# Hybrid DeltaNet / attention layer on one core: small merge matmuls in four unbroken runs a head, and an order planned with transfer issue times, one more dependence and eight transfers under way

## The chip, the core and the metric

The kernel runs on one core of a Trainium2 chip. The metric is the device time of one execution in microseconds (us), the median of several. Engines are called as the profile does: PE (TensorE matmul), PEld (its weight loads), DVE (VectorE), ACT (ScalarE), POOL (GpSimd) and SP (SyncE, which only issues transfers; ACT issues some too).

## What is computed

One layer over 1024 latent tokens and 256 context tokens of width 1024, all in 32-bit floats. Two branches are fed from one projection and merged by gates:

```python
a_mat = jnp.where(strict, einsum('nbhid,nbhjd->nbhij', kc * bc[..., None], kc) * decay, 0.0)
t_mat = lax.linalg.triangular_solve(eye + a_mat, eye, left_side=True, lower=True)
u = t_mat @ (vc * bc[..., None])
w = t_mat @ (kc * (bc * jnp.exp(gc))[..., None])
def step(s, xs_i):                       # one chunk after the other
    v_new = u_i - einsum('bhck,bhkv->bhcv', w_i, s)
    s_next = s * jnp.exp(gl_i)[..., None, None] + einsum('bhck,bhcv->bhkv', kd_i, v_new)
    o = einsum('bhck,bhkv->bhcv', qd_i, s) + einsum('bhij,bhjv->bhiv', qk_i, v_new)
...
o_b = diff_attend(q_l, concatenate([k_c, k_l]), concatenate([v_c, v_l]), lam)   # 8 heads, softmax
merged = g_a * (y_a @ w_oa) + g_b * (y_b @ w_ob)
return x + gate * (merged @ w_out)
```

Branch A is a gated delta rule, in both directions, for 8 heads. Each head needs, for every chunk, the inverse of a triangular matrix, and then a scan over the chunks. Branch B is softmax attention.

## The kernel before

The kernel works with chunks of 128 tokens, 10 a head and direction. Its stages follow each other on PE: the projection and its convolution (to some 430 us of the span), the query, key and value parts of attention with the preparation of the first two heads of the delta rule (to 756 us), the two scans of the delta rule with the rest of the preparation (to 1350 us), attention together with the projection `ma` of branch A (to 1832 us), and the last projections `mb`, `x`, `z`.

**Preparation of a head** (`gdn_prep`, line 1077 on). `gram` products and decays give the matrix `X`. Its 32x32 blocks on the diagonal go through DRAM (`da`, read back as `ab`), are inverted by 62 steps on DVE in the tile `ts` (lines 1153 and 1155), which POOL first sets to zeros and ones (lines 1146 and 1147), and are stored as `db` (line 1157, issued by SP) and read back as `RR`. Then blocks are merged, by four kinds of small matmul: 40 of 32x32 into `pz`, 60 of 32x32 into `p2` and `p3`, and, for each half of the chunks, 10 of 64x64 into `pz6` and 10 into `pu6`. A PSUM pool of two banks (`gpa`) serves these, `gram`, and the transposes `tr` and `oT`. The profile writes the tiles as `pz`, `p` and `pu`; each of these matmuls stands in the trace as two passes, as those of `chain`, `out` and `gram` do.

**Scans** (`scan`, line 1289 on). For each of two directions: `chain` matmuls on PE, scalings on ACT (`vd`, line 1318, `vn`) and DVE (`r`, line 1309, `S`, line 1331), in a ring of dependence; `out` matmuls beside it. `sets` (line 1265) loads a head's `sk`, `kk`, `vv` and `sq`, `loads` (line 1280) the `x` and `qk` of two chunks. `tails` finishes a head: `of` and the product `oa` (line 1387) on POOL, then the transposes `oT` on PE.

**Fill.** Where no scan or preparation has a matmul ready, PE is given `mm` matmuls of other projections (`fill_flow`, units of 48 matmuls of 128x512); their outputs `zo` leave PSUM on ACT (line 1031), which then issues their transfer (line 1033).

**What sets the order.** The program is written in the order that a planner in the kernel's own code finds: every part is a generator that yields an engine, a cost in us and what it waits for; `flow` (and `turn_flow` for the front and for attention) takes the part that could start first by the planner's clocks, with a bias for each part (`BIAS`, `WB`, `ABIAS`; a lower one goes first). The engines work in order, so what the planner puts ahead on an engine is waited for there.

Of the kernel before, what the change touches and what calls it, by code (L numbers as in the profile page):

```python
# [23 lines left out]
NT = LT // P  # L24
# [19 lines left out]
class Block:  # L44
    def __init__(self, ctx, tc, a):
        self.ctx, self.tc, self.nc, self.a = ctx, tc, tc.nc, a
        self.dbg = {}
        self.now = self.dq = 0.0
        self.clk, self.port = [0.0] * 5, [0.0, 0.0]
        self.table, self.heat = None, 0.0  # L50
        self.streams = []
        self.ahead = None

    def mm(self, out, lhsT, rhs, start=True, stop=True):
        self.nc.tensor.matmul(out, lhsT, rhs, start=start, stop=stop)  # L55

# [56 lines left out]
    def begin_at(self, e, ready):  # L113
        return max(self.clk[ENG[e]], ready, self.port[1] if e == DV2 else self.port[0] if e == POOL else 0.0)
# [6 lines left out]
    def step(self, s):  # L121
# [588 lines left out]
    def run(self):  # L710
# [4 lines left out]
        with ExitStack() as left:  # L715
            self.hp, self.hs = self.spool(left, "hp"), {}
            self.hgroup(0)
            with ExitStack() as lw, ExitStack() as cx:
# [21 lines left out]
                with tc.manual_schedule(engines={E.PE, E.DVE, E.Activation, E.Pool, E.SP}):  # L740
# [30 lines left out]
                    for g, b in ((self.scan(0), 0), (self.scan(1), 0), (self.forever(self.outq[0]), 1),  # L771
                                 (self.forever(self.outq[1]), 1), (self.forever(self.evacs), 2),
                                 (self.forever(self.posts[0]), 2), (self.forever(self.posts[1]), 2), (first, 3),
                                 (self.preps(1), 3), (self.tails(), 3), (self.sets(), 3), (self.loads(0), 3), (self.loads(1), 3),
                                 (self.forever(self.asides), 3)):
# [263 lines left out]
    def gdn_first(self):  # L1039
# [8 lines left out]
        self.unit_t = {}  # L1048
# [28 lines left out]
    def gdn_prep(self, h):  # L1077
# [68 lines left out]
        t1 = yield PL1, 0.89, [], lambda: nc.gpsimd.memset(ts, 0.0)  # L1146
# [10 lines left out]
        t = yield DMA, 0.91, [t], lambda: nc.sync.dma_start(self.db[h].rearrange("u m i j -> (u m) i j"), ts)  # L1157
# [24 lines left out]
        for c in range(NT):  # L1182
            for (b1, b2) in ((0, 1), (2, 3)):
                t = yield PE, 0.03, [tz, b], lambda: self.mm(p2[B(b1), c], R[B(b1), c], Z[B(b1), c]), 0.25
                t = yield PE, 0.03, [tz, b], lambda: self.mm(p2[B(b2), c], Rt[B(b2), NT + c], Z[B(b2), c]), 0.25
            t3 = yield PE, 0.02, [tz, b], lambda: self.mm(p3[B(1), c], Z[B(0), c], R[B(0), c]), 0.25
            t3 = yield PE, 0.02, [tz, b], lambda: self.mm(p3[B(2), c], Z[B(3), c], Rt[B(3), NT + c]), 0.25
# [17 lines left out]
        ends = []  # L1205
        for c0, nb in ((5, 5), (0, 5)):
            cs = slice(c0, c0 + nb)
            yield self.psum()
            b = self.banks.pop(0)
            pz = PT("pz6")[:, :nb * 64].rearrange("p (c f) -> p c f", f=64)  # L1210
            for j in range(nb):
                c = c0 + j
                t = yield PE, 0.065, [tx, b], lambda: self.mm(pz[lo, j], X[hi, 0, c, lo], X[hi, 0, c, hi]), 0.5
                t = yield PE, 0.065, [tx, b], lambda: self.mm(pz[hi, j], X[lo, 1, c, hi], X[lo, 1, c, lo]), 0.5
            tz = yield DVE, 0.398, [t], lambda: V.tensor_scalar_mul(Z6[:, cs], pz, -1.0)
# [989 lines left out]
```

## Time and profile before

| what | value |
|---|---|
| time, median of 3 runs | 2006.67 us (2004.43 to 2008.17) |
| profiled execution: its own time | 2004.12 us |
| its span, first to last instruction | 2002.3 us |
| PE busy | 1940.0 us (97%) |
| PEld busy | 1692.7 us (85%) |
| DVE, ACT, POOL busy | 1457.0, 1071.5, 673.9 us |
| mean granted clock of TensorE | 0.992 |

The profiled execution's own time is 1.8 us above its span. Ends of matmuls are modelled by the profiler, so the time from start to start tells more of PE than its busy time.

### The profile page before, as it was taken

The numbers are of one execution on the slowest core, as the hardware profiler recorded it, in microseconds if no ns is written. First come the engines' busy times: TensorE is split into PE (matmuls) and PEld (weight loads), VectorE is DVE, ScalarE is ACT, GpSimd is POOL, SyncE is SP. The second block draws the span as 40 slices with busy tenths as digits, with TensorE's granted clock in tenths as the row PEclk, the third lists the DMA queues.
The fourth block names the chain that finished last, engine by engine and source line by source line (L and its number), as shares of the span: only waits on it lengthen the run. The fifth ranks groups of instructions, "written<-read, shape, count | busy, mean of one in ns | idle before, by whom it ended". The sixth has DMA issues, their size and how long they took to land.

```text
span 2002.3 us, 37575 instructions
## 1 busy us (share of the span) xinstructions
PE 1940.0 (97%) x13807; PEld 1692.7 (85%) x13807; DVE 1457.0 (73%) x3613; ACT 1071.5 (54%) x2187; POOL 673.9 (34%) x610
## 2 busy tenths in 40 slices
PE   6999999999999999999899999999999999999999
PEld 4988888899999997878777888887788888888887
DVE  4797989858877895557556786237679999885677
ACT  4453445352325543666456754547668888874222
POOL 3200000015521422332323333334657666672203
PEclk9999999999999999999999999999999999999999
DMA  9154453575456645855664765648664575336542
GB/s 323 59 145 108 132 131 95 134 228 165 129 158 211 195 152 147 260 178 193 194 224 133 257 173 164 218 140 249 169 163 117 148 232 140 108 107 211 189 157 85
DMA packets 388415, 336.40 MB, mean 168 GB/s; under 512 B 144913, under 2 KB 331891, under 8 KB 388231
## 3 DMA queue, kind: packets, MB, share of 16 engines
q1 hardware_dynamic: 324295, 273.18, 46.3%
q10 hardware_dynamic: 63936, 60.83, 9.8%
q8 instruction: 109, 1.79, 0.4%
q14 instruction: 75, 0.61, 0.1%
HBM read 222.14 MB, written 111.79 MB: 167 GB/s over the span
## 4 chain that ended last, share of the span: by engine, by line
PE 73%; DVE 10%; DMA 8%; ACT 4%; issue 2%; SPq 1%; POOL 1%; ACTq 0%; DVEq 0%; POOLq 0%
PE mm L55 37%; PE chain L55 5%; PE v L55 5%; PE mb L55 4%; PE s L55 4%; PE ma L55 3%; PE x L55 3%; DVE S L1560 3%; PE out L55 3%; PE t L58 2%; DMA hx<-in_w_in_dram 1%; PE gram L55 1%; DVE al L1634 1%; ACT S L1573 1%; DVE ac L590 1%
## 5 line engine op out<-in xcount | busy, mean ns | idle before, releaser
L55 PE MATMUL mm<-hs,wh 128*128 128x512 f32 (+1 forms) x2048 | 648.9, 391 | 1.5 <-DVE hs L403 1.4
L55 PEld LDWEIGHTS mm<-hs,wh 128*128 128x128 f32 x2048 | 373.1, 190 | 60.3 <-DVE hs L403 2.0
L55 PE MATMUL mm<-hs,wl 128*128 128x512 f32 (+1 forms) x1024 | 400.8, 391 | 0.0
L55 PE MATMUL mm<-wh,hs 128*128 128x256 f32 (+1 forms) x1792 | 334.8, 286 | 0.0
L55 PEld LDWEIGHTS mm<-wh,hs 128*128 128x128 f32 x1792 | 281.5, 191 | 0.4
L1560 DVE TENSOR_SCALAR_CACHE_REDUCE S<-s,rsq 128x512 f32<-128x512 f32 (+1 forms) x384 | 241.9, 655 | 33.6 <-PE s L55 30.8
L55 PE MATMUL mm<-wl,hs 128*128 128x256 f32 (+1 forms) x896 | 256.0, 286 | 0.0
L55 PEld LDWEIGHTS mm<-hs,wl 128*128 128x128 f32 x1024 | 194.9, 190 | 29.1 <-issue 0.9
L1597 POOL TENSOR_TENSOR S<-S 128x1280 f32<-128x1280 f32 x64 | 188.8, 2952 | 90.2 <-ACT S L1590 87.7
L1573 ACT ACTIVATE S<-S,mn 128x1280 f32<-128x1280 f32 x128 | 174.7, 1366 | 34.5 <-DVE mn L1572 33.7
L55 PEld LDWEIGHTS mm<-wl,hs 128*128 128x128 f32 x896 | 171.2, 191 | 0.3
L590 DVE SCALAR_TENSOR_TENSOR ac<-xc,convT,ac 128x1284 f32<-128x1284 f32 (+1 forms) x96 | 138.7, 1449 | 16.3 <-ACT ac L588 15.6
L55 PE MATMUL s<-kk,qh 128*128 128x512 f32 (+1 forms) x384 | 145.3, 379 | 3.1 <-DVE S L1560 2.8
L55 PE MATMUL s<-kk,ql 128*128 128x512 f32 (+1 forms) x384 | 134.0, 360 | 0.0
L1634 DVE TENSOR_TENSOR al<-t,ah 128x512 fp32r<-128x512 f32 (+1 forms) x192 | 107.6, 593 | 10.3 <-ACT ah L1629 9.7
L1629 ACT CAST ah<-t 128x512 fp32r<-128x512 f32 (+1 forms) x192 | 90.0, 516 | 30.4 <-PE t L58 29.1
L575 POOL MEMSET xc<- 128x2 f32 (+1 forms) x64 | 3.6, 99 | 301.8 <-DMA gkk<-xc 118.0
L1153 DVE TENSOR_TENSOR tmp<-ab,ts 80x31 f32<-80x31 f32 (+15 forms) x248 | 97.2, 392 | 8.2 <-DMA ab<-da 2.6
L1331 DVE SCALAR_TENSOR_TENSOR S<-S,egl,chain 128x128 f32<-128x128 f32 x128 | 43.1, 344 | 79.8 <-PE chain L55 76.8
L578 ACT COPY xc<-mm 128x512 f32<-128x512 f32 (+1 forms) x64 | 33.4, 534 | 125.2 <-PE mm L55 101.7
L58 PE MATMUL t<-ct,S 128*128 128x128 f32 x640 | 95.8, 276 | 1.0 <-ACT zo L1031 0.5
L1318 ACT ACTIVATE vd<-chain,edk 128x128 f32<-128x128 f32 x144 | 52.2, 369 | 80.4 <-PE chain L55 75.0
(298 smaller groups left out, 4478.1 us busy)
## 6 DMA issues: line engine op xcount, KB each, us to landing
wr<-in_w_in_dram ACTq DMA_DIRECT2D x44, 512.0 KB
hx<-in_w_in_dram ACTq DMA_DIRECT2D x64, 256.0 KB
X<-gcd SPq DMA_DIRECT2D x16, 640.0 KB
kd<-col SPq DMA_DIRECT2D x40, 256.0 KB
xd<-X SPq DMA_DIRECT2D x16, 640.0 KB
x<-xd SPq DMA_DIRECT2D x80, 128.0 KB
kk<-kd SPq DMA_DIRECT2D x32, 320.0 KB
wa<-in_w_ada_dram SPq DMA_DIRECT2D x8, 1024.0 KB
```

The costliest lines, as they stand in the source:

```text
L55: self.nc.tensor.matmul(out, lhsT, rhs, start=start, stop=stop)
L58: self.nc.tensor.transpose(out, src, self.ident[:src.shape[0], :src.shape[0]])
L578: e = yield ACT, 0.57 if m == 512 else 0.31, [t, x["old"]], lambda: nc.scalar.copy(xc[:, d:d + m], pt[:, :m])
L590: t = yield DV2, 1.21e-3 * wd, [t], lambda: nc.vector.scalar_tensor_tensor(ac[:, :wd], xc[:, j:j + wd], self.convw(j, x["ct"]), ac[:, :wd] ...
L1153: t = yield DV2, n * w / 960.0 + 0.08, [t, t1], lambda: V.tensor_tensor(tv, ab[:, j + 1:, j:j + 1].to_broadcast([80, n, w]), ts[:, j, :w]. ...
L1318: td = yield ACT, 0.251, [t], lambda: nc.scalar.activation(vd, pc[:, 1], AF.Copy, scale=self.edk[:, c, g:g + 1])
L1331: t = yield DVE, 0.263, [t], lambda: V.scalar_tensor_tensor(Sn, S, self.egl[:, c, g:g + 1], pc[:, 2], ALU.mult, ALU.add)
L1560: e = yield DVE, 0.675 if m == 512 else 0.408, [e, self.sfree[c].get(n - 4 + c)], lambda: self.nc.vector.tensor_scalar(x["S"][c][:, o:o + ...
L1573: x["x"].append((yield ACT, 1.36, [e], lambda: nc.scalar.activation(S, S, AF.Exp, bias=x["mn"][:, c:c + 1], scale=-1.0, accum_out=w["l0"][ ...
L1597: e = yield POOL, 2.9, [e], lambda: self.nc.gpsimd.tensor_tensor(S0, S0, S1, ALU.add)
L1629: e = yield ACT, 0.48 if nb == 4 else 0.27, [t, y["old", k]], lambda: self.nc.scalar.copy(y["ah", k][:, :, q], pv)
L1634: t = yield DVE, 0.603 if k < 2 else 0.322, [e, y["old", k]], lambda: self.nc.vector.tensor_tensor(y["al", k][:, :, q], pv, y["ah", k][:, ...
```

## The change

The 40 matmuls into `pz`, the 60 into `p2` and `p3`, the 20 into `pz6` and the 20 into `pu6` of a head are each yielded as one piece, with one cost, so that the planner can put nothing between them; the two halves of the 64x64 steps are done together, which takes both banks of the pool at a time (`psum(2)`). The planner's model gets three terms: an issue on SP takes 0.4 us of SP instead of 0.05; a transfer is not issued before the eighth transfer back has landed (`lanes`; this holds for issues by SP and by ACT); and the zeroing of `ts` waits for the last store of `ts` (`ts_t`). `sets` loads `vv` and `kk` ahead of `sk`, and in the first head all but `vv` come after the first loads of both scans. Biases are changed: `sets` goes from 0 to -0.3, `loads` from 0 to -0.5, the fill's weights from -0.3 to -0.15, and in attention several of `ABIAS`. (`FB1` is changed too, but it is used only where 38 units of fill are done, and there are 32.)

```diff
@@ class Block
+        self.lanes = [0.0] * 8
+    def mms(self, ops):
+        for x in ops:
+            self.mm(*x)
...
     def begin_at(self, e, ready):
-        return max(self.clk[ENG[e]], ready, self.port[1] if e == DV2 else self.port[0] if e == POOL else 0.0)
+        return max(self.clk[ENG[e]], ready, self.port[1] if e == DV2 else self.port[0] if e == POOL else
+                   self.lanes[0] if e in (DMA, ADMA) else 0.0)
...
-            self.clk[e] = start + 0.05 if h[0] == DMA else keep
+            self.clk[e] = start + self.SPI if h[0] == DMA else keep
             end += self.LAND
+            self.lanes = self.lanes[1:] + [end]
@@ gdn_prep
-        t1 = yield PL1, 0.89, [], lambda: nc.gpsimd.memset(ts, 0.0)
+        t1 = yield PL1, 0.89, [self.ts_t], lambda: nc.gpsimd.memset(ts, 0.0)
...
-        t = yield DMA, 0.91, [t], lambda: nc.sync.dma_start(self.db[h].rearrange("u m i j -> (u m) i j"), ts)
+        t = self.ts_t = yield DMA, 0.91, [t], lambda: nc.sync.dma_start(self.db[h].rearrange("u m i j -> (u m) i j"), ts)
...
-        for c in range(NT):
-            for (b1, b2) in ((0, 1), (2, 3)):
-                t = yield PE, 0.03, [tt, b], lambda: self.mm(pz[B(b1), c], X[B(b2), 0, c, B(b1)], Rt[B(b2), c]), 0.25
-                t = yield PE, 0.03, [tt, b], lambda: self.mm(pz[B(b2), c], X[B(b1), 1, c, B(b2)], R[B(b1), NT + c]), 0.25
+        t = yield PE, 1.02, [tt, b], lambda: self.mms(
+            x for c in range(NT) for b1, b2 in ((0, 1), (2, 3)) for x in (
+                (pz[B(b1), c], X[B(b2), 0, c, B(b1)], Rt[B(b2), c]), (pz[B(b2), c], X[B(b1), 1, c, B(b2)], R[B(b1), NT + c]))), 0.25
...
-        for c0, nb in ((5, 5), (0, 5)):
-            cs = slice(c0, c0 + nb)
-            yield self.psum()
-            b = self.banks.pop(0)
...
+        yield self.psum(2)
+        b = [self.banks.pop(0), self.banks.pop(0)]
+        pz = [v6("pz6"), v6("pz6")]
+        t = yield PE, 1.5, [tx, b], lambda: self.mms(
+            x for cs, z in zip(halves, pz) for j in range(5) for c in (cs.start + j,) for x in (
+                (z[lo, j], X[hi, 0, c, lo], X[hi, 0, c, hi]), (z[hi, j], X[lo, 1, c, hi], X[lo, 1, c, lo]))), 0.5
...
@@ sets
-            for n, src in (("sk", self.gk[h]), ("kk", self.gkk[h]), ("vv", self.gv[h]), ("sq", self.gq[h])):
+            for n, src in (("vv", self.gv[h]), ("kk", self.gkk[h]), ("sk", self.gk[h]), ("sq", self.gq[h])):
+                if h == 0 and n == "kk":
+                    yield lambda: all((d, 0, 8) in self.units_ for d in range(2))
@@ biases
+    SPI = 0.4
-    WB = -0.3
+    WB = -0.15
-    BIAS = (0, 0, -0.3, 0, 0)
+    BIAS = dict(scan=0, outq=0, evacs=-0.3, posts=-0.3, preps=0, tails=0, sets=-0.3, loads=-0.5, asides=0)
-    ABIAS = dict(rels=-5.0, softs=-5.7, norms=3.8, gateq=-13.3, sums=-15.8,
-                 outs=-32.1, lows=-2.4, highs=-13.2, adds=30.9, scales=31.0, evs=-3.0, mouts=13.8,
-                 att_out=0.5, turns=5.3, scores=-2.6, merge=1.0)
+    ABIAS = dict(rels=-5.0, softs=-0.02, norms=6.65, gateq=-13.3, sums=-14.54,
+                 outs=-50.16, lows=-2.4, highs=-2.68, adds=26.02, scales=31.0, evs=22.29, mouts=13.8,
+                 att_out=-3.61, turns=3.19, scores=-6.47, merge=1.0)
```

The same instructions are issued before and after, but for four more table loads on ACT (33 instead of 29). What moves is seen at three places.

On PE, at the first merge that falls into the scans (head 2; `pz` is the merge, `chain` and `out` the scans, `mm` the fill). Before:

```order
L55 MATMUL pz<-RR,X 32x32 x3
L55 MATMUL chain<-S,sk 128x128
L55 MATMUL pz<-RR,X 32x32 x2
L55 MATMUL chain<-r,x 128x128
L55 MATMUL pz<-RR,X 32x32 x18
L55 MATMUL out<-S,sq 128x128
L55 MATMUL pz<-RR,X 32x32 x2
L55 MATMUL chain<-r,x 128x128
L55 MATMUL pz<-RR,X 32x32 x9
L55 MATMUL chain<-vd,kk 128x128
L55 MATMUL out<-vn,qk 128x128
L55 MATMUL out<-S,sq 128x128
```

The same merge now:

```order
L56 MATMUL chain<-S,sk 128x128
L56 MATMUL mm<-hs,wl 128x512
L56 MATMUL out<-S,sq 128x128
L56 MATMUL mm<-hs,wh 128x512
L56 MATMUL pz<-RR,X 32x32 x40
L56 MATMUL chain<-r,x 128x128
L56 MATMUL chain<-vd,kk 128x128
L56 MATMUL out<-vn,qk 128x128
```

Six pieces of `pz` with scan matmuls between them have become one piece of 40. Over the whole program the small matmuls stood in 111 pieces before (26 of `pz` 32x32, 36 of `p`, 21 of `pz` 64x64 and 28 of `pu`), and stand in 32 now (8 of each).

On POOL, where the sixth zeroing of `ts` (MEMSET, `L1146` before) meets the third head's end (`of`, then `oa<-oa,of`). Before:

```order
L1282 TENSOR_TENSOR qk<-qk,ct 128x256 x2
L172 TENSOR_TENSOR of<-of,mhalf 128x8
L1146 MEMSET ts 80x1024
L1387 TENSOR_TENSOR oa<-oa,of 128x1024
L880 TENSOR_TENSOR wl<-hx,wh 128x512
L1147 MEMSET ts 80x32
```

Now:

```order
L179 TENSOR_TENSOR of<-of,mhalf 128x8
L1394 TENSOR_TENSOR oa<-oa,of 128x1024
L887 TENSOR_TENSOR wl<-hx,wh 128x512
L1153 MEMSET ts 80x1024
L1154 MEMSET ts 80x32
L1289 TENSOR_TENSOR qk<-qk,ct 128x256 x4
```

The zeroing has gone from ahead of the product `oa` to behind it and behind a weight's split `wl`.

On SP, at the start of the scans (`qd` and `qkd` are stores of the stages before). Before:

```order
L1018 DMA qd<-col 128x2x256 x4
L1265 DMA sk<-gk 128x1280
L1265 DMA kk<-gkk 128x10x128
L1265 DMA vv<-gv 128x10x128
L1265 DMA sq<-gq 128x1024
L1280 DMA x<-xd 128x256 x2
L1280 DMA qk<-qkd 128x256
L1280 DMA x<-xd 128x256 x2
```

Now:

```order
L1025 DMA qd<-col 128x2x256 x2
L1287 DMA x<-xd 128x256 x2
L1287 DMA qk<-qkd 128x256
L1287 DMA x<-xd 128x256 x2
L1287 DMA qk<-qkd 128x256
L1272 DMA vv<-gv 128x10x128
L1272 DMA kk<-gkk 128x10x128
L1272 DMA sk<-gk 128x1280
```

The small loads of both scans go out ahead of the four large ones, of which `vv` is now the first and `sk` the third.

Of the 2688 fill and projection matmuls `mm` of 128x512, 1224 stood ahead of the first `chain` and 87 behind the last `oT`; now 1208 and 133 do, and behind the first score matmul of attention stand 90 instead of 39.

## Rows read from the trace of the kernel before

**Rows 1.** The span and the mean granted clock of the core.
```profile
core 0: 2002.3 us, clock 0.992
```

**Rows 2.** Busy time by stage: stretch of the span, its length, then busy us (and instructions) of PE, PEld, DVE, ACT and POOL, the granted TensorE clock, the share of the DMA engines and GB/s.
```profile
0.00:100.00 100.00, 81.88 (x570) 65.92 (x571) 59.85 (x98) 47.46 (x76) 28.01 (x48) 1.00 0.55 191
100.00:430.00 330.00, 328.19 (x1767) 282.70 (x1766) 275.90 (x413) 142.12 (x181) 3.85 (x55) 1.00 0.52 133
430.00:756.00 326.00, 323.28 (x3106) 316.66 (x3105) 263.03 (x671) 139.80 (x314) 117.47 (x89) 1.00 0.56 175
756.00:1350.00 594.00, 569.92 (x4689) 483.54 (x4688) 349.70 (x992) 331.16 (x957) 188.69 (x248) 0.98 0.61 189
1350.00:1440.00 90.00, 82.53 (x444) 68.97 (x443) 59.53 (x200) 60.36 (x94) 42.68 (x21) 0.94 0.79 213
1440.00:1832.00 392.00, 387.87 (x2523) 339.87 (x2522) 334.80 (x1113) 309.64 (x516) 256.29 (x129) 1.00 0.54 150
```

**Rows 3.** What PE waited for between 756 and 1350 us: us in total, times, longest.
```profile
PE chain L55 <- ACT vd L1318: 9.7, 3, 4.9
PE oT L58 <- POOL oa L1387: 5.3, 1, 5.3
PE chain L55 <- DMA qk<-qkd: 3.3, 1, 3.3
...
PE chain L55 <- DMA vv<-gv: 1.8, 2, 1.6
```

**Rows 4.** PE in order of time around an unbroken merge (head 0): start us, us from the first start to the last end of the row, instruction and count (of passes).
```profile
588.31 0.28 PE L55 MATMUL mm<-wl,hs 128*128 128x256 f32 x1
588.43 0.28 PE L55 MATMUL mm<-wh,hs 128*128 128x256 f32 x1
588.64 0.89 PE L55 MATMUL pz<-RR,X 32*32 32x32 f32 x80
589.45 0.38 PE L55 MATMUL mm<-wh,hs 128*128 128x256 f32 x1
589.68 0.28 PE L55 MATMUL mm<-wl,hs 128*128 128x256 f32 x1
```

**Rows 5.** The same view around a merge that is cut into pieces (head 2).
```profile
782.87 0.49 PE L55 MATMUL chain<-S,sk 128*128 128x128 f32 x2
783.29 0.25 PE L55 MATMUL pz<-RR,X 32*32 32x32 f32 x4
783.47 0.49 PE L55 MATMUL chain<-r,x 128*128 128x128 f32 x2
...
785.98 0.39 PE L55 MATMUL out<-vn,qk 128*128 128x128 f32 x2
786.20 0.39 PE L55 MATMUL out<-S,sq 128*128 128x128 f32 x2
```

**Rows 6.** POOL in order of time; in brackets the idle time before and what ended it.
```profile
959.89 1.65 POOL L172 TENSOR_TENSOR of<-of,mhalf 128x8 f32<-128x8 f32 x1 [6.41 <-DVE of L1384]
969.94 0.95 POOL L1146 MEMSET ts<- 80x1024 f32 x1 [8.40 <-DMA db<-ts]
970.85 1.90 POOL L1387 TENSOR_TENSOR oa<-oa,of 128x1024 f32<-128x1024 f32 x1
```

**Rows 7.** SP in order of time: issue of transfers (start us, us, which).
```profile
748.54 3.74 SPq L1265 DMA_DIRECT2D sq<-gq  x1
...
957.88 7.17 SPq L1139 DMA_DIRECT2D da<-X  x4
...
966.28 0.60 SPq L1157 DMA_DIRECT2D db<-ts  x1
```

**Rows 8.** ACT in order of time.
```profile
893.87 0.34 ACTq L1033 DMA_DIRECT2D sza<-zo  x1
894.26 2.44 ACT L1231 ACTIVATE X<-X,beta 128x128 f32<-128x128 f32 x8 [5.60 <-DMA sq<-gq]
...
1130.38 2.45 ACT L1102 ACTIVATE X<-X,gcc 128x128 f32<-128x128 f32 x8 [0.69 <-ACT zo L1031]
1132.85 1.28 ACT L1104 ACT_TABLE_LOAD   x1
```

**Rows 9.** Stretches in which the granted clock was half, in the columns of the second group.
```profile
758.60:765.40 6.80, 5.58 (x16) 4.74 (x17) 0.29 (x1) 1.76 (x4) 0.00 (x0) 0.50 0.76 184
898.50:901.90 3.40, 3.40 (x27) 2.84 (x27) 0.70 (x2) 0.00 (x0) 3.03 (x4) 0.50 0.94 300
970.20:977.00 6.80, 4.20 (x14) 3.72 (x15) 0.69 (x2) 0.00 (x0) 4.52 (x5) 0.50 1.12 210
1055.50:1058.90 3.40, 3.40 (x25) 2.58 (x23) 1.79 (x5) 2.80 (x9) 1.23 (x1) 0.50 0.00 0
1383.20:1386.60 3.40, 3.40 (x12) 2.64 (x12) 3.03 (x11) 3.40 (x6) 0.65 (x1) 0.50 0.84 268
1431.00:1437.80 6.80, 5.11 (x18) 4.43 (x19) 4.36 (x14) 4.43 (x11) 4.98 (x3) 0.50 0.50 154
```

**Rows 10.** What PE waited for between 1350 and 1440 us, the longest one.
```profile
PE v L55 <- DVE mn L1572: 4.7, 1, 4.7
```

**Rows 11.** What PE waited for between 1440 and 1832 us, the longest one.
```profile
PE s L55 <- DVE S L1560: 1.0, 3, 0.4
```

More of the change, by code (lines that the diff above doesn't have):

```diff
@@ L770, in more @@
                         yield lambda: False
[L771 to L775, printed above, removed]
+                    for g, b in ((self.scan(0), "scan"), (self.scan(1), "scan"), (self.forever(self.outq[0]), "outq"),
+                                 (self.forever(self.outq[1]), "outq"), (self.forever(self.evacs), "evacs"),
+                                 (self.forever(self.posts[0]), "posts"), (self.forever(self.posts[1]), "posts"), (first, "preps"),
+                                 (self.preps(1), "preps"), (self.tails(), "tails"), (self.sets(), "sets"), (self.loads(0), "loads"),
+                                 (self.loads(1), "loads"), (self.forever(self.asides), "asides")):
                         self.stream(g, self.BIAS[b]) if g is not first else self.streams.append([g, self.BIAS[b], head, None])
@@ L1204, in gdn_prep @@
         Z6 = T("Z6", [P, NT, 64], "w4")
-        ends = []
-        for c0, nb in ((5, 5), (0, 5)):
-            cs = slice(c0, c0 + nb)
-            yield self.psum()
-            b = self.banks.pop(0)
[L1210 to L1215, printed above, removed]
-            self.banks.append(tz)
-            yield self.psum()
-            b = self.banks.pop(0)
-            pu = PT("pu6")[:, :nb * 64].rearrange("p (c f) -> p c f", f=64)
-            for j in range(nb):
-                c = c0 + j
-                t = yield PE, 0.065, [tz, t6, b], lambda: self.mm(pu[lo, j], t64[lo, c], Z6[lo, c]), 0.5
-                t = yield PE, 0.065, [tz, t6, b], lambda: self.mm(pu[hi, j], t64[hi, c], Z6[hi, c]), 0.5
-            e = [(yield PL1, 0.38, [tz], lambda: nc.gpsimd.memset(X[hi, 0, cs, lo], 0.0)),
-                 (yield PL1, 0.38, [tz], lambda: nc.gpsimd.memset(X[lo, 1, cs, hi], 0.0))]
-            f = [(yield ACT, 0.43, [t], lambda: nc.scalar.copy(X[lo, 0, cs, hi], pu[lo])),
-                 (yield ACT, 0.43, [t], lambda: nc.scalar.copy(X[hi, 1, cs, lo], pu[hi]))]
@@ new lines, in gdn_prep @@
+        tz = []
+        for cs, z in zip(halves, pz):
+            tz += [(yield DVE, 0.398, [t], lambda: V.tensor_scalar_mul(Z6[:, cs], z, -1.0))]
+            self.banks.append(tz[-1])
+        yield self.psum(2)
+        b = [self.banks.pop(0), self.banks.pop(0)]
+        pu = [v6("pu6"), v6("pu6")]
+        t = yield PE, 1.5, [tz, t6, b], lambda: self.mms(
+            x for cs, u in zip(halves, pu) for j in range(5) for c in (cs.start + j,) for x in (
+                (u[lo, j], t64[lo, c], Z6[lo, c]), (u[hi, j], t64[hi, c], Z6[hi, c]))), 0.5
@@ L1228, in gdn_prep @@
+        for cs, u in zip(halves, pu):
+            e = [(yield PL1, 0.38, tz, lambda: nc.gpsimd.memset(X[hi, 0, cs, lo], 0.0)),
+                 (yield PL1, 0.38, tz, lambda: nc.gpsimd.memset(X[lo, 1, cs, hi], 0.0))]
+            f = [(yield ACT, 0.43, [t], lambda: nc.scalar.copy(X[lo, 0, cs, hi], u[lo])),
+                 (yield ACT, 0.43, [t], lambda: nc.scalar.copy(X[hi, 1, cs, lo], u[hi]))]
             self.banks.append(f)
+            ends = []
             for d in range(2):
-                for c in range(c0, c0 + nb):
-                    t = yield ACT, 0.263, [e, f], lambda: nc.scalar.activation(
+                for c in range(cs.start, cs.stop):
+                    t1 = yield ACT, 0.263, [e, f], lambda: nc.scalar.activation(
```

18 lines of the change are left out of this document (9 added, 9 removed).

## The prediction

> **What bounds the kernel now.** I read the stages first [rows 2]. In each of them PE is busy for nearly the whole stretch: 328.2 of 330 us in the convolution, 323.3 of 326 in the parts of attention, 387.9 of 392 in attention. PE has work of its own everywhere, because fill is put wherever a scan or a softmax is late, so the time is PE's work plus the time in which PE stands still or is clocked down. The two weak stretches are the scans (569.9 of 594 us, granted clock 0.98) and the start of attention (82.5 of 90 us, clock 0.94). The front (81.9 of 100 us) keeps its order.
>
> Then I read what PE waited for in the scans [rows 3], and, for each wait, what the engine that was waited for had been doing [rows 6 to 8]. The reader should see that these waits do not come from the scans' own arithmetic but from an engine that was held, in order, by something else. At 970 us PE waits 5.3 us for POOL's product `oa`; POOL has been standing 8.4 us before its zeroing of `ts`, for the store `db`; and SP issued `db` late, at 966.28 us, because four issues of `da` had kept it 7.17 us [rows 6, 7]. At 894 us ACT waits 5.6 us for the landing of an unrelated load, `sq`, behind which it could issue a store of its own and only then go on to `vd`, for which the scan waits [rows 3, 8]. At the scans' start SP needs 3.74 us to issue one load of 512 KB [rows 7], and PE waits 3.3 us for a load issued behind it [rows 3]. Last I read the clock: it was at its lower level, 1.2 GHz, in six stretches in and after the scans, 30.6 us in all, and the four of the scans, from 758.6, 898.5, 970.2 and 1055.5 us on, are as many as the waits of PE there that were longer than 3 us; in the third PE was busy for only 4.2 of 6.8 us [rows 3, 9].
>
> **The change, part by part.** The sum is made against the profiled execution: span 2002.3 us [rows 1], 2004.1 us by its own time, which is 2.6 us below the median of the runs.
>
> *Fewer pieces.* An unbroken merge of 80 passes takes the fill from start to start from 588.43 to 589.68 us, 1.25 us for two matmuls that alone take 0.12 us each (588.31 to 588.43): 1.01 us for 80 passes [rows 4]. A piece of 4 passes between two scan matmuls takes these from 782.87 to 783.47, 0.60 us where scan matmuls without a piece between them follow after 0.22 (785.98 to 786.20): 0.38 us for 4 passes [rows 5]. So (1.01 - 0.38) / 76 = 0.008 us is what a pass costs, and 0.38 - 4 x 0.008 = 0.35 us is what a piece costs by itself, whatever is in it: PE goes over from the full array to the small blocks and back, and the matmuls on both sides are late. The order has 111 pieces before and 32 now. 79 x 0.35 = -27.7 us, all of it time of PE, and fill takes it up at once. For the 46 of these cuts that are of 32x32 the price is measured; the other 33 are of 64x64, and their price is taken from the same row. Ends: 46 x 0.35 = -16 us if a cut of 64x64 costs nothing, and -36 us if it costs 0.6 us, the whole of the gap in row 783.47.
>
> *Planned with issue times, the store's dependence and eight transfers.* In the scans PE stood still for 594 - 569.9 = 24.1 us [rows 2]; the four stretches at half clock there last 20.4 us [rows 9], of which PE was busy 16.6, so that they cost some 8 us. Together 32 us. The three new terms are the causes that the rows show: the zeroing that held POOL (5.3 us, and with it 6.8 us of half clock), the issues on SP (3.3 and 1.8 us, and 6.8 us of half clock), and ACT's issue that waits for a landing (9.7 us in three waits, and twice 3.4 us of half clock). The order now has the zeroing behind `oa`, and the scans' first loads ahead of the large ones. But the planner still takes 0.4 us for any issue where one took 3.74 us and four took 7.17, and an order with other waits may bring others. I take half: -16 us. Ends: nothing, and -32 us.
>
> *Merges that cannot be broken.* A scan matmul that becomes ready during one now waits for up to 1.0 us, as long as the measured one takes [rows 4], and may wait longer for 64x64. 24 of the 32 pieces, those of six heads, lie in the scans. That costs nothing as long as fill is there: PE works through the merge. The cover is real: 133 `mm` of 128x512 are left behind the last `oT`, against 87 before. If it were gone, half of 24 x 1.0 us, 12 us, would come back.
>
> *Start of attention.* PE stood still for 7.5 us in 1350 to 1440 us [rows 2], 4.7 of them in one wait behind DVE's queue [rows 10], and 10.2 us ran at half clock [rows 9], some 4 us. Now 90 instead of 39 matmuls of fill are left to put into these gaps. I take a third: -4 us, with ends 0 and -11.
>
> *Attention itself.* PE stood still for only 4.1 us, and its longest kind of wait sums to 1.0 us [rows 2, 11]: nothing can be won, and a new order of an engine that is busy 334.8 of 392 us (DVE) can lose. I take +4 us, about what PE now stands still there; ends -3 and, as the rival below, much more.
>
> *Table loads on ACT.* Four more at 1.28 us [rows 8], 5 us of an engine that is busy 331 of 594 us in the scans: 0, and +5 if every one of them holds up a `vd` that PE waits for. The Trainium skill (ScalarE: Activation LUTs, section "What ACT_TABLE_LOAD costs") adds about 1.38 us of drain to each load, by which four would be some 10.6 us, an estimate from that page, and the sum 1973 if all of it were on the path. The trace does not agree: the load at 1132.85 us starts 0.02 us after the work before it ends [rows 8].
>
> Sum: -27.7 - 16 - 4 + 4 = -43.7 us, 2004.1 to 1960.4 us, and with the 2.6 us of the median **1963 us**.
>
> **The rivals.**
>
> *The counts do not fit the chip.* The merges pay, but the planner's new waits are as wrong as the old: as many us of standing still in the scans as before, elsewhere. For it: issues of 1.8 us and more, which 0.4 us does not tell of [rows 7]. Against it: the largest single waits are just those that the three terms name. Then 2006.7 - 27.7 = 1979 us.
>
> *The scans set the pace.* PE is not the limit between 756 and 1350 us but the ring of `chain`, ACT and DVE; then PE time that is saved turns into waiting, and unbroken merges hold the ring up. For it: weight loads keep PEld busy for only 483.5 of 594 us there, 81%, against 97% in the stage before [rows 2]. Against it: PE's waits there sum to 24 us, and it always has fill. Then the 27.7 us are lost, which leaves 2006.7 - 16 - 4 + 4 = 1991 us, or with the 12 us of merges on top about 2003 us, no change. The Trainium skill (Perfetto Trace Analysis, section "Identifying the Most-Contended Engine") holds that busy time of matmuls is a poor measure of how full PE is, and busy time of weight loads a good one. By that rule this rival would be the likelier; scan matmuls that follow each other without a gap (0.22 us from start to start for one of two passes) speak against it [rows 5].
>
> *Attention is slowed: slower than before.* `evs`, DVE's emptying of score banks, goes from -3 to +22.29 in the biases, behind nearly all else on DVE, which is busy 85% of that stage [rows 2]. A score matmul then finds no free bank and PE, in order, stands. The place is the score matmuls `s`; the price of a stall as the one at the start of attention is 4.7 us of standing [rows 10] and half of the 5.1 us that PE worked at half clock from 1431 us on [rows 9], 7 us a time. Six such stalls, fewer than one a head, eat the 44 us; with twelve the time is 1963 + 84 = 2047 us. Against it: PE now gets its scores in smaller portions between `t` and `ma`, which gives DVE time to empty the banks.
>
> *It does not do what it says.* If the order had hardly moved, the time would stay at 2006.7 us; the order on PE speaks against it.
>
> **How the numbers follow.** 1963 us as the sum has it, between 1944 and 1974: 0.56. The counts that do not fit, 1974 to 1990 us: 0.2. The scans' pace: 0.12, of which two thirds fall near 1991 us and one third at no change. Attention slowed: 0.1. Nothing done: 0.02. The range from 1944 to 1992 us takes in the forecast, the second case and most of the third. Its lower end is the sum with -36 instead of -27.7 and -27 instead of -16. A measurement of this kernel can tell 0.2% from no change, 4 us: faster 0.84, within it 0.06, slower 0.1.
>
> **What would show it.** In the profile of the changed kernel: 32 pieces of `pz`, `p` and `pu`, each unbroken, and no scan matmul pairs 0.60 us apart with one between; a scan stage shorter by 35 us or more at the same work; PE's waits there for `oa` and `vd` below half, and fewer than four stretches of half clock; no wait of POOL before the zeroing that holds `oa`; waits of PE for `S` in attention still about 1 us. The prediction is wrong if the scan stage is not shorter by 20 us or more, if standing still there has grown, or if attention takes more than 10 us longer for the same matmuls.

## The result, and the profile after

The changed kernel takes **1994.38 us** (median; 1993.22 to 1996.13) against 2006.19 us of before: ratio **0.9942** (95% interval 0.9924 to 0.9959). The interval leaves out 1, so it is faster, by 12 us (0.6%) and not by the 43.7 that I forecast, and it lies above my range, which ended at 1992. Executions whose mean granted clock was 0.75 or lower (three in all, at 0.39, 0.66 and 0.75) are left out of every ratio here.

The profiled execution took 1993.2 us. Its stages move: the scans now run from 762 to 1295 us, from the first `chain` to the last. The cuts of [rows 2] do not fit that: they start the scans 4 us ahead of the first `chain` and end them 22 us behind the last. So before is shown here once more, cut as the changed kernel is: from the first `gram`, from the first `chain`, from the last, and 145 us on. Columns as in [rows 2]. Before:

```profile
426.00:760.00 334.00, 327.07 (x3129) 319.90 (x3130) 263.76 (x672) 144.39 (x324) 117.47 (x89) 1.00 0.56 177
760.00:1328.00 568.00, 547.19 (x4583) 464.94 (x4584) 345.58 (x985) 320.88 (x928) 179.02 (x240) 0.98 0.62 190
1328.00:1473.00 145.00, 137.23 (x768) 116.47 (x767) 91.59 (x303) 96.97 (x166) 74.67 (x37) 0.96 0.61 171
```

Changed:

```profile
core 0: 1991.4 us, clock 0.992
```

```profile
439.00:762.00 323.00, 312.33 (x3012) 305.59 (x3012) 263.09 (x663) 140.67 (x321) 119.92 (x91) 0.99 0.54 170
762.00:1295.00 533.00, 514.24 (x4558) 447.12 (x4559) 342.61 (x993) 320.14 (x929) 178.55 (x238) 0.99 0.67 205
1295.00:1440.00 145.00, 128.80 (x661) 107.02 (x659) 71.77 (x237) 84.16 (x140) 59.36 (x31) 0.93 0.60 168
1440.00:1821.00 381.00, 374.94 (x2451) 331.34 (x2452) 323.17 (x1082) 301.87 (x503) 249.64 (x127) 1.00 0.54 151
```

The scan stage is 35 us shorter (with 25 matmul passes fewer in it), and PE stands still a little less in it (18.8 us, against 20.8). But the preparation ahead of it now has 10.7 us of standing still instead of 6.9, and the start of attention 16.2 instead of 7.8. Busy time is too coarse for the terms of the sum, since ends of matmuls are modelled. So I also counted **losses**: for every matmul the time from its start to the next one's start, less the median that before shows for its shape. These medians sum to 1873.8 us in every kernel, so what is left over is all of the difference. "Pieces" are the small merge matmuls and the matmul on either side of them; the other columns are everything else in that stage, standing still, half clock and small delays together. Which neighbour goes to which column, under half clock above all, can move 2 us between pieces and scans.

| loss, us | front | convolution, preparation | pieces | scans | attention and after | sum |
|---|---|---|---|---|---|---|
| before | 18.0 | 9.4 | 25.9 | 36.8 | 28.7 | 118.8 |
| changed | 16.8 | 17.5 | 3.9 | 28.6 | 40.3 | 107.1 |
| difference | -1.2 | +8.1 | -22.0 | -8.2 | +11.6 | -11.7 |

Of the 3.9 us that are left at the pieces, 3.3 are one stop inside the second merge of head 2, between 784.65 and 787.91 us, for which the profile names no engine and no transfer:

```profile
787.91 0.21 PE L56 MATMUL p<-Z,RR 32*32 32x32 f32 x1 [3.07 <-issue]
```

In the three other kernels with this order (old_abias, wq_after and wq_old_abias below) PE stops at the same matmul, for 3.0 to 3.7 us; why, no run shows. It is not the price of a cut.

The merges run as written. Around the first one in the scans (PE in order of time, as [rows 4, 5]) 80 passes take 0.81 us from start to start, and the ring's next matmuls follow at once:

```profile
781.33 0.48 PE L56 MATMUL mm<-hs,wh 128*128 128x512 f32 x1
781.74 0.89 PE L56 MATMUL pz<-RR,X 32*32 32x32 f32 x80
782.55 0.49 PE L56 MATMUL chain<-r,x 128*128 128x128 f32 x2
782.88 0.39 PE L56 MATMUL chain<-vd,kk 128*128 128x128 f32 x2
```

In the scans PE's waits of [rows 3] have shrunk: `vd` 3.3 us for 9.7, and `oa`, 5.3 us before, is gone from the list (what PE waited for from 762 to 1295 us: us in total, times, longest):

```profile
PE chain L56 <- ACT vn L1329: 4.1, 3, 2.9
PE p L56 <- issue: 3.6, 3, 3.1
PE chain L56 <- ACT vd L1325: 3.3, 3, 1.5
PE chain L56 <- DMA vv<-gv: 3.0, 2, 2.0
```

What came in their place lies elsewhere. The same view of the preparation (439 to 762 us):

```profile
PE tr L63 <- DVE fin L1001: 3.1, 3, 2.4
PE gram L56 <- DVE X L1132: 1.7, 1, 1.7
PE gram L56 <- DMA kq<-gk: 1.7, 2, 1.2
PE tr L63 <- POOL fin L1009: 1.5, 1, 1.5
```

and all engines' waits at attention's start, from 1330 to 1345 us:

```profile
ACT wh L886 <- DMA hx<-in_w_in_dram: 8.0, 1, 8.0
DVE wl L887 <- ACT wh L886: 6.4, 1, 6.4
...
PE s L56 <- DVE S L1568: 5.9, 1, 5.9
```

That is one chain. ACT stands, in order, at a weight cast `wh` whose load has not landed; DVE stands at `wl`, which needs `wh`; behind `wl` stands the emptying of a score bank, for which PE's `s` waits. ACT issued the load at 1323.93 us and it landed at 1341.02, 17.1 us later; in that time the DMA engines were 99% busy, and four issues of `ql` held SP for 11.56 us (ACT, then SP, then the stretch):

```profile
1323.93 0.39 ACTq L882 DMA_DIRECT2D hx<-in_w_in_dram  x1
...
1341.02 0.62 ACT L886 CAST wh<-hx 128x512 fp32r<-128x512 f32 x1 [8.01 <-DMA hx<-in_w_in_dram]
```

```profile
1329.90 11.56 SPq L1514 DMA_DIRECT2D ql<-qd  x4
```

```profile
1319.00:1341.00 22.00, 16.24 (x75) 12.85 (x73) 7.98 (x30) 5.20 (x7) 6.50 (x3) 1.00 0.99 248
```

Half clock moved the same way: as many stretches as in [rows 9] and about as long together (30.7 us), but two in the scans instead of four, one in the preparation (440.3 us), and the three longest in attention's start:

```profile
1341.40:1348.30 6.90, 5.21 (x13) 4.23 (x14) 4.95 (x18) 6.84 (x9) 0.00 (x0) 0.51 0.92 224
1372.20:1379.00 6.80, 6.37 (x27) 5.89 (x28) 5.01 (x17) 4.94 (x7) 0.00 (x0) 0.50 0.91 297
1419.90:1426.80 6.90, 6.14 (x19) 4.79 (x20) 5.36 (x18) 5.69 (x9) 6.82 (x4) 0.51 0.27 77
```

Together this accounts for the start of attention. In the 145 us from the last `chain` on PE stands 8.4 us longer than in before, and half clock costs half of the busy time in those three stretches, 8.9 us, where before has two, of 4.3: 13 us. Cut behind the first sixth of its `v` matmuls, attention lost 14.7 us there and 14.1 in the rest before, and now 28.5 and 11.8. So all of the +11.6 us, and more, is at the start. Its size is not fixed by the order alone: old_bias below, with the same order on PE in attention, lost 21.6 and 13.3 us.

### The profile page after: what moved, and what is told of

Read it like the earlier page. It is cut to its first block, busy times and chain, and to the rows that moved or that the text cites. A ratio compares the mean times of both kernels' runs of the same rounds, so it can differ in the third digit from the quotient of the medians.

```text
span 1991.4 us, 37572 instructions
## 1 busy us (share of the span) xinstructions
PE 1915.2 (96%) x13807; PEld 1683.4 (85%) x13807; DVE 1449.1 (73%) x3613; ACT 1075.3 (54%) x2191; POOL 676.4 (34%) x610
## 3 DMA queue, kind: packets, MB, share of 16 engines
q1 hardware_dynamic: 324295, 273.18, 46.6%
## 4 chain that ended last, share of the span: by engine, by line
PE 71%; DVE 11%; DMA 9%; ACT 5%; issue 2%; SPq 2%; POOL 1%; ACTq 0%; DVEq 0%; POOLq 0%
PE mm L56 37%; PE chain L56 5%; PE mb L56 4%; PE v L56 4%; PE s L56 4%; PE ma L56 3%; PE x L56 3%; DVE S L1568 2%; PE out L56 2%; PE t L63 2%; DMA hx<-in_w_in_dram 2%; DVE al L1642 1%; DMA sk<-gk 1%; PE gram L56 1%; ACT S L1581 1%
## 5 line engine op out<-in xcount | busy, mean ns | idle before, releaser
L1162 DVE TENSOR_TENSOR ts<-ts,tmp 80x31 f32<-80x31 f32 (+15 forms) x248 | 91.5, 369 | 5.6
L56 PEld LDWEIGHTS s<-kk,qh 128*128 128x128 f32 x384 | 73.7, 192 | 25.1 <-DVE S L1568 14.9
```

What stands on the lines that cost most here:

```text
L1162: t = yield DV2, n * w / 960.0 + 0.08, [t, t1], lambda: V.tensor_tensor(ts[:, j + 1:, :w], ts[:, j + 1:, :w], tv, ALU.subtract)
```

## The experiments

All of them in one table: ratio to executions of before taken beside it, and losses as above, counted in one profile each. The profiled execution is one of several: in no_plan and hyb10 it was 7 us below its kernel's median, in old_bias 6 us above, in all others within 4.

| kernel | ratio (95%) | preparation | pieces | scans | attention |
|---|---|---|---|---|---|
| before | 1 | 9.4 | 25.9 | 36.8 | 28.7 |
| changed | 0.9942 (0.9924 to 0.9959) | 17.5 | 3.9 | 28.6 | 40.3 |
| m_only | 1.0039 (1.0020 to 1.0058) | 11.9 | 0.8 | 40.8 | 54.3 |
| no_m | 1.0009 (0.9990 to 1.0028) | 15.0 | 26.4 | 24.2 | 34.8 |
| old_abias | 1.0003 (0.9988 to 1.0018) | 16.0 | 6.3 | 27.2 | 53.3 |
| plan_look (= plan_only) | 1.0180 (1.0149 to 1.0211) | 14.1 | 35.3 | 30.2 | 60.5 |
| score_bias | 0.9983 (0.9971 to 0.9996) | 9.0 | 26.0 | 34.1 | 28.8 |
| b_new_abias | 1.0021 (1.0009 to 1.0033) | 10.8 | 28.4 | 37.8 | 35.2 |
| old_bias | 0.9948 (0.9929 to 0.9968) | 15.6 | 5.2 | 46.6 | 34.9 |
| no_plan | 0.9912 (0.9894 to 0.9930) | 11.1 | 4.0 | 32.2 | 34.0 |
| m_score | 0.9954 (0.9937 to 0.9971) | 16.1 | 0.7 | 40.9 | 35.6 |
| m_new | 0.9919 (0.9899 to 0.9939) | 15.4 | 1.1 | 41.5 | 26.9 |
| hyb10 | 0.9919 (0.9899 to 0.9939) | 9.6 | 3.2 | 33.9 | 33.5 |
| plan_score | 1.0058 (1.0042 to 1.0075) | 13.1 | 35.6 | 30.7 | 31.9 |
| wq_after | 0.9901 (0.9886 to 0.9915) | 17.3 | 5.4 | 24.6 | 35.2 |
| wq_old_abias | 0.9976 (0.9964 to 0.9987) | 15.9 | 7.1 | 28.9 | 48.7 |
| wq_m_new | 0.9932 (0.9911 to 0.9953) | 12.7 | 0.5 | 42.3 | 32.1 |
| late | 0.9922 (0.9902 to 0.9941) | 8.1 | 6.9 | 45.3 | 29.5 |
| wq_no_plan | 0.9889 (0.9872 to 0.9907) | 12.4 | 4.3 | 35.3 | 31.9 |

How far one profile can be trusted shows where kernels share an order. The changed kernel, old_abias, wq_after and wq_old_abias have the same order on PE up to attention: 24.6 to 28.9 us in the scans, 15.9 to 17.5 in the preparation. The four m_ kernels share another: 40.8 to 42.3 and 11.9 to 16.1. In attention the two pairs with one order each (changed and old_bias, wq_after and late) differ by 5 to 6 us, so that of the changed kernel's 40.3 us some 5 may belong to this one profile.

With means over kernels of one order the parts can be told apart better. In the scans the planner's terms gained 5.8 us without the rest of the change (plan_look and plan_score against before, score_bias and b_new_abias) and 6.5 with it (the changed kernel's four against no_plan, hyb10 and wq_no_plan). In the preparation they lost 3.9 and 5.6 us in the same pairs: over these two stages together they are worth some 1 to 2 us. The unbroken merges by themselves (the four m_ kernels against before's three) lost 5.1 us in the scans and 4.3 in the preparation.

**One part each.** First theory: the pieces pay as forecast, and the planner's terms or the new biases lose it again; rival: the unbroken merges themselves make the new waits.

**m_only**: before, with the diff's `mms` and `gdn_prep` merges.

> The kernel before with nothing but the unbroken merges (32 pieces instead of 111). In the traces the time lost at the pieces went from 25.9 to 3.9 us. Theory A (the pieces pay 22 us, the loss of the whole change lies in the planner's terms and biases): 2006 - 22 = 1984 us, stalls in the preparation about as before (8 us). Theory B (unbroken merges that hold both banks make the new waits for gram and tr themselves): 1994 to 2000 us, with more than 12 us of stalls and half clock in the preparation. Theory C (the loss lies in attention's biases alone): as A here.

Measured 2011.64 us: slower than before. The pieces gave 25.1 us, as the theories had it, but attention lost 25.6 us more, and the scans 4. No theory had put the loss there.

**no_m**: the changed kernel with the merges of before.

> The changed kernel with the merges of before (100 pieces again). Theory A: 68 pieces more at 22/79 = 0.28 us, 1994 + 19 = 2013 us, with the preparation's stalls of the changed kernel still there. Theory B: 1990 to 2000 us, since the new waits go with the runs. Theory C: as A.

Measured 2007.63 us, 13 us above the changed kernel: nearer to theory A, and above all that theory B allows. The pieces cost 22.5 us again; scans and attention are 4 and 5 us better, which is no more than profiles of one order differ by.

**old_abias**
```diff
-    ABIAS = dict(rels=-5.0, softs=-0.02, norms=6.65, ...
+    ABIAS = dict(rels=-5.0, softs=-5.7, norms=3.8, ...
```

> The changed kernel with the attention biases of before; the order up to the start of attention is the same. Theory C (the new biases cost what attention lost, 11 us of standing still and half clock): 1983 us, and no wait of PE over 3 us for S behind DVE. Theory A with the loss spread over the planner's terms: 1991 to 1997 us, since the long wait for S at 1336.8 us comes from a late load of weights.

Measured 2007.22 us, the other way: attention lost 53.3 us. The new biases gain 13 us in the changed kernel. They do so behind the start: cut as above, attention lost 14.8 and 38.5 us here, against 28.5 and 11.8 in the changed kernel. At the start they lose. From the last `chain` to the first sixth of attention PE waited 0.4 us for `S` here, and 10.0 us in the changed kernel.

**plan_only**: before, with `lanes`, `SPI` and `ts_t`.

> The kernel before with the planner's three terms alone (0.4 us an issue, eight transfers, the zeroing behind the store), merges broken (117 pieces), old biases. My prediction: 2006 - 16 = 1990 us. Theory A (the terms only move the waits, some into preparation and attention): 2004 to 2018 us. Theory B (the terms gain, the runs lose): 1990 us.

Measured 2042.01 us (ratio 1.0172, 1.0144 to 1.0200), worse than any theory had it. It was run once more for its profile:

> The planner's three terms alone once more, which were 36 us slower than before, for a profile at full clock. Theory K (most of it is attention again: an order of attention under the old biases that fits badly, as with the unbroken merges alone): scans at 25 to 37 us of standing still, half clock and small losses, where before has 37, attention at 55 us or more, where before has 29. Rival (the terms hurt where they act): scans or preparation worse by 20 us or more.

Again 2042.84 us. The scans lose 30.2 us instead of 36.8, so the terms do help there; but attention loses 60.5, 32 more than before, and the pieces (117 now) 9 more, of which 5 are four stops of 0.7 to 1.7 us at them. One of attention's waits, ACT from 1546 us on:

```profile
1555.07 0.59 ACT L1633 CAST ah<-t 128x512 fp32r<-128x512 f32 x1 [4.66 <-PE t L59]
1562.25 0.62 ACT L1782 CAST wh<-wq 128x512 fp32r<-128x512 f32 x1 [6.59 <-DMA wq<-in_w_oa_dram]
1562.78 0.58 ACT L1633 CAST ah<-t 128x512 fp32r<-128x512 f32 x1
```

Again `wh` stands on ACT before its load has landed, with `ah` behind it, for which PE's `v` waits 5.4 us.

**Is it the edit, or the order?** Three quite different edits had cost attention some 25 to 32 us under the old biases. Two theories: old biases fitted to one start of attention, so that any other order loses; or scatter, each order with its own loss.

**score_bias** (in before):
```diff
-                 att_out=0.5, turns=5.3, scores=-2.6, merge=1.0)
+                 att_out=0.5, turns=5.3, scores=-2.4, merge=1.0)
```

> The kernel before with one number of attention's biases changed by 0.2 (scores from -2.6 to -2.4). Everything up to attention keeps its order; in attention 1708 of the 2824 matmuls of s, t, v, ma and m stand elsewhere. Theory D (the old biases were fitted to one start of attention, and any other order of attention costs 10 us or more, whatever moved it): 2015 to 2030 us, all of the difference in attention. Theory E (unbroken merges hurt attention by what they leave behind, not by moving its order): 2003 to 2009 us.

Measured 2003.82 us, attention 28.8: a very different order that loses as little. "Any other order loses" falls.

**m_score** is m_only with that line, **plan_score** is plan_only with it.

> Unbroken merges alone, with one attention bias moved by 0.2 (scores from -2.6 to -2.4), which moves 1286 of 2824 matmuls in attention and nothing ahead of it. Theory J (the 25 us that attention lost with the unbroken merges are scatter of its order, and another order loses another amount): attention loses 28 to 42 us, 1986 to 2000 us. Theory I (after unbroken merges attention under the old biases always loses some 54 us): 2008 to 2016 us.

> The planner's three terms alone, which took 2042 us with 60 us lost in attention, with one attention bias moved by 0.2 (scores from -2.6 to -2.4): 2060 of 2824 matmuls of attention stand elsewhere, nothing ahead of it moves. If the 60 us were the scatter of one order: attention loses 28 to 42 us and the time is 2010 to 2025 us. If the planner's terms themselves harm attention: 50 us or more, 2032 to 2045 us.

Both came back: 1995.98 us (attention 35.6 instead of 54.3) and 2017.19 us (31.9 instead of 60.5). What PE waited for from 1440 us on, in plan_look and then in plan_score:

```profile
PE v L56 <- ACT ah L1633: 5.4, 1, 5.4
PE v L56 <- DVE oT L1675: 4.3, 7, 1.6
PE t L59 <- POOL S L1601: 2.6, 2, 2.0
PE ma L56 <- DVE g L1812: 1.6, 1, 1.6
```

```profile
PE t L59 <- POOL S L1601: 1.6, 3, 0.6
PE v L56 <- DVE oT L1675: 1.2, 4, 0.6
```

So most of the 25 to 32 us was neither the merges' nor the terms' effect on attention. An edit without meaning, one bias moved by 0.2, takes 19 and 29 us of them away: they belong to the one order that each edit happened to lead to.

**Biases.** **b_new_abias**: before with the new `ABIAS`. **m_new**: m_only with it.

> The kernel before with the attention biases of the changed kernel and nothing else. Theory D: these biases are fitted to the changed kernel's start of attention, so 2010 to 2030 us here. Theory C (the new biases are better in themselves, by the 13 us that they give the changed kernel): 1993 us.

> The kernel before with the unbroken merges and the new attention biases, nothing else of the change. If the terms add up as the profiles so far have them: pieces 1 to 4 us, scans 41, preparation 12, attention 34 (as in the three other kernels with these biases): 2006 - 25 + 4 + 3 + 6 = 1994 us. If the planner's terms are needed for attention to start well: 2005 us or more.

2014.29 and 1990.38 us. The same biases that gain 13 us in the changed kernel cost before some 4 us. The sum for m_new (1994) held within 4 us: the pieces' 25 us are all there at last, since attention in this order loses as little as in before. In the ten kernels that have the new biases all through attention lost 26.9 to 40.3 us, in the eight with the old ones 28.7 to 60.5. The cut behind the first sixth parts the two: the rest of attention lost 11.7 to 13.3 us in all ten, and 12.1 to 41.2 in the eight; the start 14.8 to 28.5 in the ten, and 14.7 to 19.5 in the eight. The new biases keep the rest of attention from scattering, and at the start they can lose.

**old_bias**: the changed kernel with `sets` loading in the order of before, and
```diff
-    WB = -0.15
-    BIAS = dict(..., sets=-0.3, loads=-0.5, asides=0)
+    WB = -0.3
+    BIAS = dict(..., sets=0, loads=0, asides=0)
```

> The changed kernel with the old biases and order of the loads in the stages before attention (sets, loads, fill's weights); attention's order is the same as in the changed kernel. Attention should lose the same there (40 us of standing still and half clock, within 5). Theory F (the new biases of these stages make the waits for gram in the preparation): preparation back at 8 us, 1988 us in all. Theory G (the planner's eight transfers make them): preparation still at 14 us, scans at 22 to 31 us for want of the new order of loads, 1994 to 2003 us.

1998.89 us. Preparation 15.6 us, so these biases do not make its waits. The scans lose 46.6 instead of 28.6 us in this profile, beyond both theories. But the profiled execution is 6 us above its kernel's median, and as a whole the kernel is only 4.5 us slower than the changed one by the medians, with intervals that overlap: that the biases and order of the loads are worth 18 us in the scans is not shown. Attention, in the same order on PE, lost 34.9.

**no_plan**: the changed kernel without the three terms.
```diff
-                   self.lanes[0] if e in (DMA, ADMA) else 0.0)
+                   0.0)
-    SPI = 0.4
+    SPI = 0.05
-        t1 = yield PL1, 0.89, [self.ts_t], lambda: nc.gpsimd.memset(ts, 0.0)
+        t1 = yield PL1, 0.89, [], lambda: nc.gpsimd.memset(ts, 0.0)
```

> The changed kernel without the planner's three terms (issues at 0.05 us, no limit of transfers, zeroing free of the store). Theory H (the terms give the 9 us that the scans gained): the scans back at 31 us of standing still and half clock, the preparation at 8 us if they made its waits, attention in an order that differs by 944 matmuls and so 0 to 15 us worse: 1994 to 2015 us. Rival (the terms do nothing): 1990 to 1998 us, scans at 22 us.

1991.21 us, if anything faster than with them, by overlapping intervals: the scans are 3.6 us worse, preparation and attention 6.4 and 6.3 us better.

**hyb10**: no_plan, with the old biases as `ABIAS0`, and
```diff
-        self.entry[n][1] = self.ABIAS.get(n, 0) + self.DUE * i
+        self.entry[n][1] = (self.ABIAS0 if i < 10 else self.ABIAS).get(n, 0) + self.DUE * i
```

> The changed kernel without the planner's three terms (1991 us), with the old attention biases for the first 10 of 64 tiles and the new ones from there on. In the profiles the first sixth of attention lost 14 to 17 us under the old biases and 21 to 27 under the new ones in all but one; the rest 12 to 14 us under the new ones, and 12 to 39 under the old. If these two parts can be joined: first sixth 14 to 17, rest 12 to 14, 1984 us. If the start is scatter too, or the hand-over makes waits of its own: 1988 to 1998 us.

1989.8 us and 33.5 us lost in attention, against 34.0 in no_plan: the two parts were not joined. Attention's first sixth came to 17.6 us, the rest to 15.9, each above what it was to be.

**Weight loads that land late, and terms that act late.** wq_after, wq_old_abias, wq_m_new and wq_no_plan are the changed kernel, old_abias, m_new and no_plan, each with
```diff
-                rs.append((r, (yield DMA, 0.73, [free[s]], lambda: ...)))
+                rs.append((r, self.later((yield DMA, 0.73, [free[s]], lambda: ...), 3.0)))
```

> The changed kernel, with the planner believing that the weight loads wq of attention land 3 us later than it thought (4.4 us measured from issue to landing, up to 7.5, where it plans 3.2). 186 of 2824 matmuls of attention move. If wh, waiting on ACT for wq, is a common cause of attention's loss: ACT's waits for wq (7.0 us) go, and with them 3 to 8 us, 1987 to 1991 us. If not: 1992 to 1998 us.

> The changed kernel with the old attention biases (2007 us, 53 us lost in attention; at 1523 us PE waited 4.8 us for ah, which stood on ACT behind wh, which waited 6.0 us for wq), with wq planned 3 us later; 1173 matmuls of attention move. If that wait is the cause: no wait of ACT for wq over 2 us, and attention loses 28 to 40 us, 1983 to 1995 us. If the loss lies in the order otherwise: 45 us or more, 2000 to 2010 us.

> Unbroken merges and the new attention biases (1990 us, 27 us lost in attention), with wq planned 3 us later; 1631 matmuls of attention move. If the late loads are a common cause: 22 to 27 us lost, 1985 to 1990 us. If any new order draws its loss anew: 27 to 40 us, 1990 to 2003 us.

1986.98 us, with ACT's wait for `wq` down from 7.0 to 2.0 us; 2001.76 us, in the other theory's range, but with a wait for `wq` of 6.3 us left, so that it tells nothing of the cause; 1992.13 us, as the rival had it. One of three by the theory. And the wait is there in the kernels that lose least under the old biases too: ACT waits 7.7 us for `wq` in before and 10.7 in score_bias, which lose 28.7 and 28.8 us. By itself it does not make the loss.

> The changed kernel without the planner's three terms (1991 us, 34 us lost in attention, one wait of 6.5 us of ACT for wq), with wq planned 3 us later; 1643 matmuls of attention move. If late weight loads are a cause by themselves: attention 27 to 31 us, 1984 to 1988 us. If any new order draws its loss anew: 27 to 40 us, 1984 to 1997 us; over 42 us would say that the new biases scatter as widely as the old.

1986.02 us, 5 us less than no_plan with intervals that overlap; attention, at 31.9 us, is only 2 us better, within what one profile can tell and outside the 27 to 31 of the theory. It is the fastest of all, and its interval does not touch the changed kernel's.

**late**: wq_after with
```diff
-                   self.lanes[0] if e in (DMA, ADMA) else 0.0)
+                   self.lanes[0] if e in (DMA, ADMA) and getattr(self, "merge", 0) >= 2 else 0.0)
-            self.clk[e] = start + self.SPI if h[0] == DMA else keep
+            self.clk[e] = start + (self.SPI if getattr(self, "merge", 0) >= 2 else 0.05) if h[0] == DMA else keep
```

> The changed kernel with wq planned 3 us later (1987 us), and with the issue times and the limit of eight transfers only from the end of the second head's merges on; attention's order is the same as there. If the terms make the preparation's waits: preparation and convolution lose 9 to 12 us instead of 17, scans and attention within 5 us of what they lost (25 and 35), 1979 to 1984 us. If not: 1985 to 1990 us.

Half right. Preparation loses 8.1 instead of 17.3 us: in this kernel its new waits come from the order that the terms make there. They are not the only way to such waits: the m_ kernels, without the terms, lose 11.9 to 16.1 us there, where before's order loses 9.0 to 10.8. But the scans drew another order, which loses 45.3 us instead of 24.6, and the time is 1992.42 us.

## Why the prediction was wrong, step by step

- **Fewer pieces: right.** -27.7 us forecast with ends -16 and -36, -22.0 measured, and -25.1 and -22.5 in the two pairs that differ in the merges alone. Without the stop of 3.3 us inside a merge the changed kernel's own figure is -25.3 as well. A cut costs 25.3 / 79 = 0.32 us, not 0.35. The merges for themselves do not make the kernel faster, though (m_only).
- **Planned with issue times, the store and eight transfers: right in kind, half in size.** -16 us forecast, -8.2 measured in the scans. The waits named went: `oa` from 5.3 us to none, `vd` from 9.7 to 3.3, four half-clock stretches to two. What I did not price: the unbroken merges cost the scans some 5 us (the m_ kernels), and the three terms by themselves are worth only some 6 (plan_look and plan_score; no_plan and its like). The rest of what no_m gains, 12.6 us, would be the order and biases of the loads; old_bias points there, but does not show the size.
- **Preparation: put at nothing without a reason, +8.1 us.** This step failed too. I costed the terms only where they were to help. They act on every stage: `late` shows that in the preparation they harm, and there the 4 to 6 us that they cost eat most of the 6 that they gain in the scans.
- **Start of attention -4, attention +4: this step failed. The two came to +11.6 us, and in single variants to +32.** At the start I had 90 matmuls of fill close gaps. Instead the loss there rose from 14.7 to 28.5 us, 8.5 of it in one chain: a weight load that landed after 17.1 us held ACT, ACT held DVE, and DVE held the score banks. For attention itself I said that PE stood still so little there that "nothing can be won", and took the order's loss as a small constant. In the changed kernel that held (14.1 to 11.8 us), in the variants under the old biases it did not: it was a property of before's order. Edits that move the planner's clocks draw a new one: seven variants lie above 35 us, before's 28.7 is near the lowest. The ends that I gave the two terms, -14 to +4 but for a rival with a chance of 0.1, should have reached up to some +32.
- **The rival "attention is slowed"** had the right place and one right chain: score banks behind DVE, 5.9 us of standing and then 5.2 us of work at half clock, which makes 8.5 us where I had put 7 us a time. In part it had the right cause too: at the start PE waits 10.0 us for `S` with the new biases and 0.4 with the old (old_abias). Whether `evs` among them does it was not run alone, and the longest of these waits goes through the late load. In the rest of attention the new biases gain 27 us, which the rival did not see.
- **The rival "scans set the pace"**, which gives nearly the measured time (1991 us), is not what happened; that its number is near is chance. The saving in the pieces was not turned into waiting in the scans, whose other losses fell as well, and the scan stage became 35 us shorter.
- Of my own tests the first two came out for the forecast (a scan stage 35 us shorter, 30 of them by the losses, with less standing still). The third (attention more than 10 us longer for the same matmuls) says wrong, and that is where it is wrong.

**Open:** what in an order makes attention lose 30 or 60 us. `wh` on ACT ahead of its load is behind long waits of PE in two of the bad orders (old_abias, plan_look from 1440 us on) and in the changed kernel, but before and score_bias have it too, and moving it helped in some only.

## What to carry to other kernels

Where a planner writes the order, an edit has two effects: what it does where it acts, and a new draw of the order everywhere behind it. Count the second as a range of its own, sized by an edit without meaning (one bias by a little): here 19 and 29 us in attention (m_score, plan_score), as much as the gain of the largest single part. In the scans, orders that only the planner's terms in an earlier stage set apart differed by 21 us (wq_after, late). And judge a change to such a kernel part by part with losses per stage; the sum alone would have said that merging (m_only) and planning (plan_only) both harm, when both help at the place that they were meant for.

## What the runs showed of the hardware

- Breaking a run of small matmuls costs 0.32 to 0.33 us a cut (25.1 us for 79 in m_only, 22.5 us for 68 in no_m); small passes in a run follow each other after some 0.01 us (80 in 0.81 us).
- A load of 256 KB that lands after 4.6 us in the median took 17.1 us while the DMA engines were 99% busy. The same fullness, at the same 248 GB/s, at attention's start in before (1350 to 1372 us) cost PE nothing, 22.00 of 22 us busy. So full DMA engines alone did not cost time; in the changed kernel the late load did, through what stood behind it on ACT and DVE.
- Four issues held SP for 11.56 us then, 2.9 us each, against the 0.4 us of the planner.
